# Copies of the identity into PSUM tiles at norms, write strengths' columns and latent vectors

## The chip, the cores and the metric

The kernel runs on one core of a Trainium2 chip. The metric is the device time of one execution in microseconds (us), and the time of a kernel is the median of its runs. A core has a matmul engine (TensorE, PE in the profile; its weight loads have a row of their own, PEld), three engines for element-wise work (VectorE is DVE, ScalarE is ACT, GpSimd is POOL) and a queue engine that issues most of the transfers (SyncE is SP). The engines run their own instruction streams in order and wait for each other by semaphores. Matmul results go to PSUM, all other data on chip stand in SBUF.

## What is computed

The input is a sequence of 256 tokens with 1024 features, all in float32. Two blocks follow one another. The first has a gated delta rule layer and a latent attention layer, each with a SwiGLU layer behind it; the second has two layers with four small mixers each and a SwiGLU layer with a causal convolution behind each. In short:

```python
def first_block(x, ...):
    for i in range(2):
        h = rms_norm(x, norm_mix[i])
        mix = gdn_mixer(h, ...) if i == 0 else mla_mixer(h, positions, ...)
        x = x + mix
        x = x + swiglu(rms_norm(x, norm_ffn[i]), ffn_w_gate_up[i], ffn_w_down[i])
    return rms_norm(x, final_norm)

def gdn_mixer(h, ...):
    proj = h @ w_in                 # q, k, v through a convolution, z, b, a
    beta = sigmoid(b)               # write strengths
    g = -exp(a_log) * softplus(a + dt_bias)   # decays, summed up along a chunk
    ...

def mla_mixer(h, ...):
    c_q, c_kv, k_rope = split(h @ w_in)       # 384, 256 and 64 columns: latent vectors
    q  = rms_norm(c_q, q_norm_g) @ w_q_up
    kv = rms_norm(c_kv, kv_norm_g) @ w_kv_up
    ...
```

The second block's norms are the same, with a scale and a shift per feature that come from a condition vector.

## The kernel before

The 256 tokens stand in two halves of 128 (t = 0 and 1), tokens on partitions. The layers run as stages one after the other: `g` (gated delta rule), `f0` (SwiGLU), `a` (latent attention), `f1` (SwiGLU), `m0` (mixers), `f2` (convolution and SwiGLU), `m1`, `f3`. In the profiled execution they begin at about 0, 298, 484, 598, 788, 968, 1180 and 1361 us.

Every large matmul is made of three: each operand is split into a high and a low part (`h_hi`, `h_lo` for activations, `wh`, `wl` for weights), and high times high, low times high and high times low are added in PSUM. `mm3_a` (L480, L483) has the weights as the stationary operand, `mm3_b` (L492 to L494) the activations. Weights are streamed: SP loads a raw 128x1024 tile, ACT makes `wh` of it (L464), and DVE (L469) or POOL (L467), as a table says, makes `wl`.

A norm works in this way for each half t. The sums of squares come from ACT, a Newton iteration of small instructions on DVE (L527 to L534) gives `rstd`, and DVE makes `xn` in two pieces of 512 columns (L601). TensorE transposes each piece into a PSUM tile `ps_t` of four 128x128 blocks (L611, transposes with the identity `ident`). In `m0`, `f2`, `m1` and `f3`, where a shift is added, it first puts the shift into the tile by one matmul with 512 columns (L604) and adds the blocks with plain float32 matmuls (L609). ACT reads the tile to make `h_hi` (L614) and DVE to make `h_lo` (L615), and the next stage's matmuls (`ps_gt` in the SwiGLU stages, `ps_ck` and `ps_cq` in `a`, `ps_lk` in `m1`) read those. One plain float32 matmul of the program is two matmuls in the trace, and a transpose is one.

In `g`, DVE makes the running sums of the decays, `gc`, by a scan (L854); four small matmuls (L896 for `beta`, L897 for `gc`) turn them and the write strengths into columns of the tile `ps_bg`, which DVE copies out (L898, L899). Between them in TensorE's queue stand the projection's matmuls into `ps_g`.

In `a`, the latent vectors of half t stand in the PSUM tiles `ps_ck` and `ps_cq`. ACT sums their squares (L1253), a Newton iteration on DVE (L507 to L521) gives `m_rs`, DVE scales both into `cn` (L1256), TensorE transposes five blocks (L1259, into `ps_ct`), ACT and DVE split them into `ck` and `cq` (L1189, L1190), and the values `ps_v` follow.

The order on each engine comes from a scheduler that places the instructions of the program by their dependencies and by priorities: a block under `high_priority(n)` moves ahead of its place (the first half of a norm does, by `np` of the stage's plan), and under `issue_after(x)` an instruction is not placed before x. All PSUM tiles named here come from one pool, `pm`.

Of the kernel before, what the change touches and what calls it, by code (L numbers as in the profile page):

```python
# [37 lines left out]
        w='PPPVPPPPPVPPPPPVPPPPPVPPPPPVPPPPPVPPPPPVPPPPPVPPPPVPPPVPPPVVVVVVV',  # L38
        pre=3,
        out=(0, 4, True),  # L40
# [337 lines left out]
class Prog:  # L378
    def __init__(self, ctx, tc, ap):
        self.tc, self.nc, self.ap = tc, tc.nc, ap  # L380
        nc = self.nc
        self.const = ctx.enter_context(tc.tile_pool(name="const", bufs=1, reuse_waits="tile"))
        self.xp = ctx.enter_context(tc.tile_pool(name="xp", bufs=1, reuse_waits="tile"))
        self.raw = ctx.enter_context(tc.tile_pool(name="raw", bufs=RAWB, reuse_waits="tile"))
        self.wsp = ctx.enter_context(tc.tile_pool(name="wsp", bufs=WSB, reuse_waits="tile"))
        self.hp = ctx.enter_context(tc.tile_pool(name="hp", bufs=1, reuse_waits="tile"))
        self.sm = ctx.enter_context(tc.tile_pool(name="sm", bufs=3, reuse_waits="tile"))
        self.pa = ctx.enter_context(tc.tile_pool(name="pa", bufs=4, space=PSUM, reuse_waits="tile"))
        self.dr = ctx.enter_context(tc.tile_pool(name="dr", bufs=1, space=DRAM))
        self.nw = 0  # L390
        self.more = None
        self.ready = []
        self.last_copy = self.last_raw = None
        self.mods = {}
        self.rstd = {}
        self.scaled = {}
        self.ada_todo = [(l, c) for l in range(2) for c in range(24)]
        self.ada_held = None
        self.behind = None
        self.spare = []  # L400

        self.ident = self.const.tile([128, 128], F32, name="ident")
        make_identity(nc, self.ident)
        self.small = self.const.tile([128, SMALL.n], F32, name="small")
        self.one = self.const.tile([128, 1], F32, name="one")
        nc.vector.memset(self.one, 1.0)
        self.nhalf = self.const.tile([128, 4], F32, name="nhalf")
        nc.vector.memset(self.nhalf, -0.5)
# [63 lines left out]
    def mm3_a(self, ps, w, kt, width, m0, m, x):  # L472

        nc = self.nc
        (wh, wl), (xh, xl) = w, x
        n = 0
        last = 3 * kt - 1
        for k in range(kt):
            for xx in (xh, xl):
                nc.tensor.matmul(ps, wh[:, k * width + m0 : k * width + m0 + m], xx[:, k, :], start=(n == 0), stop=(n == last))  # L480
                n += 1
        for k in range(kt):
            self.last_mm = nc.tensor.matmul(ps, wl[:, k * width + m0 : k * width + m0 + m], xh[:, k, :], start=False, stop=(n == last))  # L483
            n += 1

    def mm3_b(self, ps, lhs, w, sl, start, stop, shared=False):

        nc = self.nc
        wh, wl = w
        xh, xl = lhs  # L490
        kw = dict(skip_group_check=True) if shared else {}
        nc.tensor.matmul(ps, xh, wh[:, sl], start=start, stop=False, **kw)  # L492
        nc.tensor.matmul(ps, xl, wh[:, sl], start=False, stop=False, **kw)  # L493
        nc.tensor.matmul(ps, xh, wl[:, sl], start=False, stop=stop, **kw)  # L494

    def rsqrt(self, out, src, shape, scale, eps, pool=None, tag=None, bufs=1, key=""):

# [90 lines left out]
    def _norm(self, x, h, l, shift, xns):  # L588
        nc = self.nc
        with ExitStack() as st:  # L590
# [3 lines left out]
            for t in range(2):  # L594
# [4 lines left out]
                with self.tc.high_priority(self.plan["np"]) if t == 0 and self.plan["np"] else ExitStack():  # L599
                    for i, hv in enumerate(halves):  # L600
                        nc.vector.scalar_tensor_tensor(xn[:, hv], scaled[i] if scaled else x[:, t, hv], rstd, self.row[:, hv], op0=ALU.mult, op1=ALU.mult)  # L601
                        ps = self.pm.tile([128, 4, 128], F32, name="ps_t", tag="mm")
                        if shift:
                            nc.tensor.matmul(ps, self.row[:, D:], self.ident[:, 4 * i : 4 * i + 4].unsqueeze(2).to_broadcast([128, 4, 128]), start=True, stop=False, skip_group_check=True)  # L604
                        for j in range(4):
# [175 lines left out]
    def _gdn_core(self, x, dr, gi, vb, rq, zs, inner):  # L781
# [105 lines left out]
        with tc.tile_pool(name="g_rk", bufs=1, reuse_waits="tile") as pr:  # L887
# [2 lines left out]
            next(kp)  # L890

            ps = self.pm.tile([128, 2, 2, 16], F32, name="ps_bg", tag="mm")
            with tc.issue_after(self.last_mm.ins):
                for n in range(2):
                    sl = slice(n * 128, n * 128 + 128)
                    nc.tensor.transpose(ps[:, 0, n, :], beta[:, sl], self.ident[0:16, 0:16])  # L896
                    nc.tensor.transpose(ps[:, 1, n, :], gc[:, sl], self.ident[0:16, 0:16])  # L897
# [294 lines left out]
    def mla(self, x):  # L1192
        nc, tc, ap = self.nc, self.tc, self.ap
        with ExitStack() as fs:
# [50 lines left out]
            for t in range(2):  # L1245
# [5 lines left out]
                with tc.high_priority(MP):  # L1251
# [3 lines left out]
                    for i, (ps, n, gain, dst) in enumerate(parts):  # L1255
                        nc.vector.tensor_scalar(cn[i][:, : n * 128], ps, rs[:, i : i + 1], None, op0=ALU.mult)  # L1256
                        pt = self.pm.tile([128, n, 128], F32, name="ps_ct", tag="mm")
                        for k in range(n):
                            nc.tensor.transpose(pt[:, k, :], cn[i][:, k * 128 : k * 128 + 128], self.ident)  # L1259
                        self.split_t(pt, n, gain, dst[0][:, :, tk], dst[1][:, :, tk])  # L1260
# [1021 lines left out]
```

## Time and profile before

| what | value |
|---|---|
| median of 3 runs | 1563.18 us (1561.58 to 1564.20) |
| the profiled execution | 1564.72 us |
| its span in the trace | 1563.0 us |
| TensorE's mean granted clock in it | 0.976 |
| PE busy, share of the span | 1456.9 us, 93% |
| DVE, ACT, POOL busy | 1080.7, 811.3, 680.6 us |

The span is the time from the first to the last instruction in the trace; the 1.7 us that the execution took beyond it lie around it. TensorE is busy for 93% of the span, and the rest is spread over some dozens of waits of a few microseconds. Its clock has two levels, 2.4 GHz (1.00 in the tables) and 1.2 GHz (0.50); the trace shows which was granted in a stretch.

### The profile page before, as it was taken

Reading aid. Unit: us, or ns where it says so; the run is one execution under the profiler, and the core shown is the slowest. Engines: PE = TensorE matmul, PEld = TensorE weight load, DVE = VectorE, ACT = ScalarE, POOL = GpSimd, SP = SyncE. Lnnn points to the kernel's source line nnn. Section 1 sums busy time; section 2 is a strip of 40 time slices with the busy share of each in tenths; the row PEclk is TensorE's granted clock in tenths of the full one; section 3 lists DMA queues with packets and bytes.
Section 4 is the critical chain, followed back from the end, with each engine's and each line's share of the span. In section 5 each row is a group of like instructions: output and inputs, shape, how many; then the busy total and the mean of one; then the engine's idle time right before and its main releaser. Section 6 shows DMA issues by size and latency. Waiting matters only on the chain.

```text
span 1563.0 us, 25562 instructions
## 1 busy us (share of the span) xinstructions
PE 1456.9 (93%) x9582; PEld 1284.4 (82%) x9582; DVE 1080.7 (69%) x2094; ACT 811.3 (52%) x1476; POOL 680.6 (44%) x471
## 2 busy tenths in 40 slices
PE   5999999899999899999998989998999797999998
PEld 4988887699987787999877766898888675699987
DVE  3587646777677566997477577788975866776652
ACT  4675555544543464554355664555544465566651
POOL 3566734245442431543145432365535523236530
PEclk9999999999999999999999999999999998999999
DMA  4655522677784455888544314777764441375550
GB/s 160 228 169 171 188 83 71 212 282 285 285 315 132 136 175 185 320 317 297 185 138 139 110 60 126 269 255 261 279 239 153 137 115 55 122 257 177 196 186 37
DMA packets 104300, 293.34 MB, mean 188 GB/s; under 512 B 28104, under 2 KB 39024, under 8 KB 98032
## 3 DMA queue, kind: packets, MB, share of 16 engines
q1 hardware_dynamic: 94928, 237.51, 45.0%
q10 hardware_dynamic: 8896, 53.14, 9.3%
q8 instruction: 75, 1.23, 0.3%
q0 software_dynamic: 352, 1.06, 0.2%
q14 instruction: 49, 0.40, 0.1%
HBM read 288.43 MB, written 3.24 MB: 187 GB/s over the span
## 4 chain that ended last, share of the span: by engine, by line
PE 54%; DVE 12%; DMA 5%; issue 4%; ACT 4%; POOL 3%; SPq 0%; ACTq 0%; POOLq 0%; DVEq 0%
PE ps_gu L480 15%; PE ps_gu L483 7%; PE ps_o L493 7%; PE ps_o L494 7%; PE ps_o L492 7%; DVE wl L469 3%; ACT wh L464 1%; POOL wl L467 1%; DVE gu_u L2236 1%; DVE ada_raw L1402 1%; DMA raw<-in_u_gu 1%; DMA ada_raw<-in_ada 1%; DVE xn L601 1%; PE ps_bs L1991 1%; DMA raw<-in_f_gu 1%
## 5 line engine op out<-in xcount | busy, mean ns | idle before, releaser
L467 POOL TENSOR_TENSOR wl<-raw,wh 128x1024 fp32r<-128x1024 f32 (+4 forms) x162 | 401.3, 2484 | 381.5 <-ACT wh L464 340.9
L464 ACT CAST wh<-raw 128x1024 fp32r<-128x1024 f32 (+3 forms) x421 | 423.6, 1018 | 247.5 <-PE ps_o L493 95.9
L469 DVE TENSOR_TENSOR wl<-raw,wh 128x1024 fp32r<-128x1024 f32 (+2 forms) x259 | 355.8, 1382 | 113.8 <-ACT wh L464 113.0
L480 PE MATMUL ps_gu<-h_hi,wh 128*128 128x256 f32 x1280 | 314.1, 283 | 8.0 <-DVE gu_u L2236 8.0
L480 PE MATMUL ps_gu<-h_lo,wh 128*128 128x256 f32 x1280 | 313.7, 283 | 0.0
L480 PEld LDWEIGHTS ps_gu<-h_hi,wh 128*128 128x128 f32 x1280 | 245.6, 192 | 8.8 <-issue 8.7
L480 PEld LDWEIGHTS ps_gu<-h_lo,wh 128*128 128x128 f32 x1280 | 245.8, 192 | 0.2
L1402 DVE CUSTOM_DVE_ANT_0 ada_raw<-ada_raw,ada_cond 128x1024 f32<-128x1024 f32 x96 | 170.9, 1795 | 65.6 <-DMA ada_raw<-in_ada 65.6
L483 PE MATMUL ps_gu<-h_hi,wl 128*128 128x256 f32 x1280 | 179.2, 283 | 3.3 <-POOL wl L467 3.2
L483 PEld LDWEIGHTS ps_gu<-h_hi,wl 128*128 128x128 f32 x1280 | 164.2, 191 | 4.2 <-POOL wl L467 3.9
L493 PE MATMUL ps_o<-wh,act_l 128*128 128x512 f32 x352 | 138.6, 394 | 0.0
L494 PE MATMUL ps_o<-wl,act_h 128*128 128x512 f32 x352 | 138.5, 394 | 0.0
L492 PE MATMUL ps_o<-wh,act_h 128*128 128x512 f32 x352 | 138.2, 393 | 0.0
L2236 DVE SCALAR_TENSOR_TENSOR gu_u<-ps_gu,f2s,gu_u 128x254 f32<-128x254 f32 (+1 forms) x176 | 81.3, 476 | 40.8 <-ACT gu_u L2234 38.8
L744 POOL TENSOR_TENSOR act_l<-gu_t,act_h 128x256 fp32r<-128x256 f32 x44 | 54.9, 1250 | 108.5 <-ACT act_h L743 108.5
L2239 POOL TENSOR_TENSOR gu_t<-gu_t,gu_u 128x256 f32<-128x256 f32 x44 | 49.2, 1118 | 85.7 <-DVE gu_u L2236 83.0
L494 PEld LDWEIGHTS ps_o<-wl,act_h 128*128 128x128 f32 x352 | 66.1, 188 | 15.3 <-issue 0.5
L492 PEld LDWEIGHTS ps_o<-wh,act_h 128*128 128x128 f32 x352 | 66.1, 188 | 15.1 <-issue 0.2
L493 PEld LDWEIGHTS ps_o<-wh,act_l 128*128 128x128 f32 x352 | 66.1, 188 | 14.9 <-issue 0.2
L480 PE MATMUL ps_g<-h_hi,wh 128*128 128x256 f32 x256 | 66.2, 294 | 1.5 <-ACT wh L464 1.5
L743 ACT CAST act_h<-gu_t 128x256 fp32r<-128x256 f32 x44 | 17.7, 406 | 96.0 <-DVE gu_t L742 96.0
L2240 ACT CAST act_h<-gu_t 128x256 fp32r<-128x256 f32 x44 | 17.9, 407 | 94.8 <-POOL gu_t L2239 94.5
(663 smaller groups left out, 2976.4 us busy)
## 6 DMA issues: line engine op xcount, KB each, us to landing
ada_raw<-in_ada ACTq DMA_DIRECT2D x48, 1024.0 KB, 6.8
raw<-in_f_gu SPq DMA_DIRECT2D x88, 512.0 KB, 4.8
raw<-in_u_gu SPq DMA_DIRECT2D x88, 512.0 KB, 4.4
raw<-in_f_dn SPq DMA_DIRECT2D x44, 512.0 KB, 5.5
raw<-in_u_dn SPq DMA_DIRECT2D x44, 512.0 KB, 4.3
raw<-in_g_qkv SPq DMA_DIRECT2D x32, 512.0 KB, 3.5
raw<-in_g_z SPq DMA_DIRECT2D x16, 512.0 KB, 4.6
raw<-in_g_out SPq DMA_DIRECT2D x16, 512.0 KB, 3.5
```

What stands on the lines that cost most here:

```text
L464: self.last_copy = nc.scalar.copy(wh[:, :cols], raw[:, :cols])
L467: nc.gpsimd.tensor_tensor(wl[:, :cols], raw[:, :cols], wh[:, :cols].bitcast(F32), op=ALU.subtract)
L469: nc.vector.tensor_tensor(wl[:, :cols], raw[:, :cols], wh[:, :cols].bitcast(F32), op=ALU.subtract)
L480: nc.tensor.matmul(ps, wh[:, k * width + m0 : k * width + m0 + m], xx[:, k, :], start=(n == 0), stop=(n == last))
L483: self.last_mm = nc.tensor.matmul(ps, wl[:, k * width + m0 : k * width + m0 + m], xh[:, k, :], start=False, stop=(n == last))
L492: nc.tensor.matmul(ps, xh, wh[:, sl], start=start, stop=False, **kw)
L493: nc.tensor.matmul(ps, xl, wh[:, sl], start=False, stop=False, **kw)
L494: nc.tensor.matmul(ps, xh, wl[:, sl], start=False, stop=stop, **kw)
L744: nc.gpsimd.tensor_tensor(al[:, m, :], t, ah[:, m, :].bitcast(F32), op=ALU.subtract)
L1402: nc.vector.tensor_tensor_reduce(raw[:, j], raw[:, j], self.cond, 1.0, 0.0, op0=ALU.mult, op1=ALU.add, accum_out=mod[:, i : i + 1])
L2236: nc.vector.scalar_tensor_tensor(u[:, j, d:], ps[:, j, : S - d], cw[:, 3 * q + 2 - d : 3 * q + 3 - d], u[:, j, d:], op0=ALU.mult, op1=ALU.add)
L2239: nc.gpsimd.tensor_tensor(t, t, u[:, 0], op=ALU.mult)
```

## The change

A new helper `busy` issues n matmuls whose two operands are the identity, into a PSUM tile that is written again right after; nothing reads what they wrote. `self.last_any` is the last matmul that `mm3_a` or `mm3_b` has issued in program order, and the copies are not placed ahead of it. They stand at three kinds of place:

- each norm, ahead of the first transposes of t = 0: 8 copies of 128x128. The first norm of the program has no matmul before it and gets none, so there are 7 such places (`f0`, `a`, `f1`, `m0`, `f2`, `m1`, `f3`);
- the write strengths' columns, ahead of the four matmuls into `ps_bg`: 12 copies of 128x64;
- the latent vectors, ahead of the first transposes of t = 0 into `ps_ct`: 17 copies of 128x128.

That is 85 matmuls of the program, all plain float32.

```diff
         for k in range(kt):
-            self.last_mm = nc.tensor.matmul(ps, wl[...], xh[:, k, :], start=False, stop=(n == last))
+            self.last_mm = self.last_any = nc.tensor.matmul(ps, wl[...], xh[:, k, :], start=False, stop=(n == last))
...
-        nc.tensor.matmul(ps, xh, wl[:, sl], start=False, stop=stop, **kw)
+        self.last_any = nc.tensor.matmul(ps, xh, wl[:, sl], start=False, stop=stop, **kw)
+
+    def busy(self, out, n, after):
+
+        w = out.shape[-1]
+        with self.tc.issue_after(after.ins):
+            for _ in range(n):
+                self.nc.tensor.matmul(out, self.ident, self.ident[:, :w], start=True, stop=True, skip_group_check=True)
...
                         ps = self.pm.tile([128, 4, 128], F32, name="ps_t", tag="mm")
+                        if t == i == 0 and self.last_any:
+                            self.busy(ps[:, 0, :], 8, self.last_any)
                         if shift:
...
             ps = self.pm.tile([128, 2, 2, 16], F32, name="ps_bg", tag="mm")
+            self.busy(ps.rearrange("p a b c -> p (a b c)"), 12, self.last_mm)
             with tc.issue_after(self.last_mm.ins):
...
                         pt = self.pm.tile([128, n, 128], F32, name="ps_ct", tag="mm")
+                        if t == i == 0:
+                            self.busy(pt[:, 0, :], 17, self.last_any)
                         for k in range(n):
                             nc.tensor.transpose(pt[:, k, :], cn[i][:, k * 128 : k * 128 + 128], self.ident)
```

The scheduler places some neighbours anew. TensorE's queue in `g`, at the write strengths' columns, has before:

```order
L483 MATMUL ps_g<-h_hi,wl 128x256 x8
L896 MATMUL ps_bg<-ident,beta 128x16
L480 MATMUL ps_g<-h_hi,wh 128x256
L897 MATMUL ps_bg<-ident,gc 128x16
L896 MATMUL ps_bg<-ident,beta 128x16
L480 MATMUL ps_g<-h_lo,wh 128x256
L897 MATMUL ps_bg<-ident,gc 128x16
L480 MATMUL ps_g<-h_hi,wh 128x256
```

and now (L480 has become L481, L896 has become L907):

```order
L484 MATMUL ps_g<-h_hi,wl 128x256 x8
L502 MATMUL ps_bg<-ident 128x64 x12
L907 MATMUL ps_bg<-ident,beta 128x16
L908 MATMUL ps_bg<-ident,gc 128x16
L907 MATMUL ps_bg<-ident,beta 128x16
L908 MATMUL ps_bg<-ident,gc 128x16
L481 MATMUL ps_g<-h_hi,wh 128x256
```

The copies stand behind the group of `ps_g` that came before, the four small matmuls behind the copies, and the two matmuls of the next group that stood among them are behind them now.

TensorE's queue in `a`, at the latent vectors of t = 0 (`ps_ck` and `ps_cq` here are the last products of t = 1), has before:

```order
L494 MATMUL ps_ck<-wl,h_hi 128x320
L492 MATMUL ps_cq<-wh,h_hi 128x384
L1259 MATMUL ps_ct<-ident,cn 128x128 x2
L493 MATMUL ps_cq<-wh,h_lo 128x384
L494 MATMUL ps_cq<-wl,h_hi 128x384
L1259 MATMUL ps_ct<-ident,cn 128x128 x3
L492 MATMUL ps_ck<-wh,h_hi 128x320
L493 MATMUL ps_ck<-wh,h_lo 128x320
L494 MATMUL ps_ck<-wl,h_hi 128x320
L492 MATMUL ps_cq<-wh,h_hi 128x384
L493 MATMUL ps_cq<-wh,h_lo 128x384
L494 MATMUL ps_cq<-wl,h_hi 128x384
```

and now:

```order
L493 MATMUL ps_ck<-wh,h_hi 128x320
L494 MATMUL ps_ck<-wh,h_lo 128x320
L495 MATMUL ps_ck<-wl,h_hi 128x320
L493 MATMUL ps_cq<-wh,h_hi 128x384
L494 MATMUL ps_cq<-wh,h_lo 128x384
L495 MATMUL ps_cq<-wl,h_hi 128x384
L502 MATMUL ps_ct<-ident 128x128 x17
L1272 MATMUL ps_ct<-ident,cn 128x128 x5
```

Before, eight products of t = 1 stood behind the first transposes; now all of them stand ahead of the copies, and the five transposes follow in one piece.

At the norm of `f3`, TensorE's queue has before, in one piece at t = 0:

```order
L604 MATMUL ps_t<-ident,row 128x512 x4
L609 MATMUL ps_t<-ident,xn 128x128 x8
```

and now, at t = 0:

```order
L502 MATMUL ps_t<-ident 128x128 x8
L614 MATMUL ps_t<-ident,row 128x512
L619 MATMUL ps_t<-ident,xn 128x128 x4
L614 MATMUL ps_t<-ident,row 128x512
L619 MATMUL ps_t<-ident,xn 128x128 x4
```

The four shift matmuls, which stood together ahead of t = 0, are now one ahead of each piece, two of them at t = 1. The norms of `f2` and `m1` change alike (three shift matmuls and one a little later in `f2`), and in `a` and `m0` the last matmuls of the stage before, which stood among the transposes or the shift matmuls, now stand ahead of the copies.

## Rows read from the trace of the kernel before

**Rows 1.** The page's first part: busy time, share of the span, instructions.

```profile
PE 1456.9 (93%) x9582; PEld 1284.4 (82%) x9582; DVE 1080.7 (69%) x2094; ACT 811.3 (52%) x1476; POOL 680.6 (44%) x471
```

**Rows 2.** Stretches: start:end, length, busy per engine (instructions), granted clock, DMA share, GB/s.

```profile
320.00:484.00 164.00, 164.00 (x1182) 154.81 (x1181) 119.45 (x123) 71.08 (x102) 81.42 (x43) 1.00 0.76 279
1000.00:1120.00 120.00, 108.71 (x890) 107.13 (x889) 110.43 (x146) 65.16 (x109) 73.90 (x48) 0.97 0.72 262
1380.00:1540.00 160.00, 160.00 (x1161) 152.21 (x1160) 98.13 (x134) 93.25 (x145) 74.64 (x55) 1.00 0.55 180
```

**Rows 3.** The same view, stretches in which the granted clock is half.

```profile
45.30:52.20 6.90, 5.58 (x25) 5.28 (x26) 4.05 (x10) 2.05 (x4) 0.17 (x1) 0.51 0.59 198
301.30:304.80 3.50, 3.50 (x12) 2.52 (x11) 2.86 (x9) 2.48 (x5) 0.00 (x0) 0.51 0.53 199
315.00:318.40 3.40, 3.40 (x9) 2.64 (x8) 0.64 (x1) 1.92 (x2) 0.00 (x0) 0.50 0.95 299
519.80:526.60 6.80, 5.36 (x18) 4.88 (x19) 4.44 (x23) 2.56 (x9) 0.24 (x1) 0.50 0.20 60
608.50:612.00 3.50, 3.50 (x11) 2.51 (x10) 1.58 (x3) 3.47 (x4) 0.00 (x0) 0.51 0.80 295
```

**Rows 4.** PE's timeline: start, duration, line, operands, shape, count [idle before, releaser].

```profile
120.66 0.51 PE L868 MATMUL pss<-fi,sq 128*128 128x16 f32 x4
...
970.67 3.60 PE L604 MATMUL ps_t<-ident,row 128*128 128x512 f32 x8
974.52 2.05 PE L609 MATMUL ps_t<-ident,xn 128*128 128x128 f32 x16 [0.25 <-DVE xn L601]
```

**Rows 5.** PE's timeline at the write strengths' columns in `g`.

```profile
41.92 1.12 PE L483 MATMUL ps_g<-h_hi,wl 128*128 128x256 f32 x8
...
46.62 0.28 PE L897 MATMUL ps_bg<-ident,gc 16*128 16x16 f32 x1 [3.11 <-DVE gc L854]
...
50.82 1.71 PE L483 MATMUL ps_g<-h_hi,wl 128*128 128x256 f32 x8
52.37 0.28 PE L480 MATMUL ps_g<-h_hi,wh 128*128 128x256 f32 x1
```

**Rows 6.** Timelines of PE and DVE at the latent vectors in `a`.

```profile
521.24 0.69 PE L1259 MATMUL ps_ct<-ident,cn 128*128 128x128 f32 x2 [5.77 <-DVE cn L1256]
...
524.76 0.63 PE L492 MATMUL ps_v<-wh,ck 128*128 128x512 f32 x1
...
528.52 1.07 PE L1259 MATMUL ps_ct<-ident,cn 128*128 128x128 f32 x5
...
514.95 1.60 DVE L507 TENSOR_SCALAR rs_v<-m_ss 128x2 f32<-128x2 f32 x1 [4.12 <-ACT cn L1253]
...
525.62 0.17 DVE L507 TENSOR_SCALAR rs_v<-m_ss 128x2 f32<-128x2 f32 x1 [0.46 <-ACT cn L1253]
```

**Rows 7.** Timelines of PE and DVE at the norm of `f0`.

```profile
300.86 1.69 PE L611 MATMUL ps_t<-ident,xn 128*128 128x128 f32 x8 [2.22 <-DVE xn L601]
...
313.67 0.63 PE L611 MATMUL ps_t<-ident,xn 128*128 128x128 f32 x4 [2.18 <-DVE xn L601]
...
308.14 5.38 DVE L601 SCALAR_TENSOR_TENSOR xn<-x_t,rstd,row 128x512 f32<-128x512 f32 x2
```

**Rows 8.** PE's timeline at the norms of `a`, `f1`, `m0`, `m1` and `f3`.

```profile
503.53 0.42 PE L494 MATMUL ps_ck<-wl,h_hi 128*128 128x320 f32 x1 [1.06 <-DVE wl L469]
...
597.83 1.03 PE L611 MATMUL ps_t<-ident,xn 128*128 128x128 f32 x8
...
607.14 1.32 PE L611 MATMUL ps_t<-ident,xn 128*128 128x128 f32 x8 [1.82 <-DVE xn L601]
...
797.69 1.49 PE L609 MATMUL ps_t<-ident,xn 128*128 128x128 f32 x11 [2.49 <-DVE xn L601]
...
1185.46 2.05 PE L609 MATMUL ps_t<-ident,xn 128*128 128x128 f32 x16 [0.58 <-DVE xn L601]
...
1365.29 2.42 PE L609 MATMUL ps_t<-ident,xn 128*128 128x128 f32 x16 [0.30 <-DVE xn L601]
```

More of the change, by code (lines that the diff above doesn't have):

```diff
@@ L392, in __init__ @@
         self.ready = []
+        self.last_any = None
         self.last_copy = self.last_raw = None
@@ L482, in mm3_a @@
         for k in range(kt):
-            self.last_mm = nc.tensor.matmul(ps, wl[:, k * width + m0 : k * width + m0 + m], xh[:, k, :], start=False, stop=(n == last))
+            self.last_mm = self.last_any = nc.tensor.matmul(ps, wl[:, k * width + m0 : k * width + m0 + m], xh[:, k, :], start=False, stop=(n == last))
             n += 1
```

## Prediction

> **What bounds the kernel now.** I read the page's first part first: TensorE is busy for 1456.9 of 1563.0 us [rows 1], so whatever is gained or lost must show up on TensorE, as idle time, as slow time, or as added work. Then I read long stretches of the SwiGLU stages: in `f0` and from 1380 us on TensorE is busy for all of 164.00 and 160.00 us [rows 2], so a shift in time ahead of these stages, in either direction, goes through them to the end. `f2` is different: between 1000 and 1120 us TensorE is busy for 108.71 and VectorE for 110.43 of 120 us [rows 2], so a microsecond more or less on TensorE just before it can vanish there. Third, the granted clock. It falls to its lower level in five stretches near the places that the change touches [rows 3]: once behind the write strengths' columns (6.90 us long), twice in `f0` (3.50 and 3.40), once behind the latent vectors (6.80) and once in `f1` (3.50). In each of them TensorE has just waited, or is waiting, for VectorE: 3.11 us for `gc` [rows 5], 2.22 and 2.18 us for `xn` [rows 7], 5.77 us for `cn` [rows 6], 1.82 us for `xn` [rows 8]. So each wait is paid twice: as idle time, and then as slow matmuls. The copies can save only the second part: they do nothing to make `gc`, `xn` or `cn` come earlier.
>
> **The price of a copy.** Sixteen plain float32 matmuls of 128x128 (8 of the program) take 2.05 us, and their starts lie about 0.118 us apart [rows 4]. So 8 copies are 1.9 us and 17 are 4.0 us of TensorE's time. For the 64-column copies no row has the shape. From below the four matmuls with 16 columns bound it, at 0.51 us or some 0.11 us apart [rows 4]; from above the 128-column pitch of 0.118. I take 0.11, since so few columns leave the weight load as the limit: 24 matmuls in 2.65 us (2.6 to 2.85). A shift matmul (L604, two in the trace) is a quarter of 3.60 us, 0.9 us [rows 4]. The seven norms, 17 and 12 copies add up to 20.0 us of TensorE's time; the question is how much of that lies in waits.
>
> **Write strengths' columns.** The group of `ps_g` ahead ends at about 43 us (it starts at 41.92 and is 1.12 long), and `gc` releases TensorE at 46.62 [rows 5]. The copies fill 2.65 of that and are over by 45.7: they cost nothing. The next group of `ps_g` runs in the slow stretch. Eight of its matmuls take 1.71 us there and 1.12 at the full clock [rows 5]; the difference is over seven distances, 0.084 us each, so 24 matmuls lose 2.0 us. If the clock stays up, the group that starts at 52.37 starts 2.0 us earlier. The four small matmuls also come ahead of the group, so the columns are copied out a little earlier. What is late next is the decay chain of the gated delta rule, which waits on other engines now and then; I keep −2.0 and allow 0 to −2.5, since a part can be lost in these waits, and another order in `g` can cost as well.
>
> **`f0`.** The copies (298.6 to 300.5) fit in the wait of 2.22 us, which ends at 300.86 [rows 7]. The slow stretch behind it [rows 3] costs up to half its length, 1.7 us. But t = 1 takes this back: its two `xn` pieces take 5.38 us on VectorE from 308.14 on, and TensorE waits 2.18 us for the second, to 313.67 [rows 7]. That time is VectorE's and the weight split's beside it; a faster TensorE only waits longer. I take 0 (−1.0 to +1.5; the upper end if a longer wait also makes the second slow stretch longer).
>
> **`a`, the norm.** Here `xn` was there before TensorE was free: the transposes stood among the last products of the stage before, and there is no wait to fill. So 1.9 us of copies lie bare. Next on the path is the wait of 1.06 us for a `wl` tile at 503.53 [rows 8], which takes most of that back. +0.5 (0 to +1.6).
>
> **`a`, the latent vectors.** The wait of 5.77 us lasts from 515.47 to 521.24 [rows 6]. Eight products of t = 1 stood behind the first transposes; they take about 1.2 us at full clock and now fill the head of the wait. The 17 copies then take 4.0 us: 515.5 + 1.2 + 4.0 = 520.7, just before `cn` is there. Behind it, between 521.24 and 524.76, before had those products and the five transposes at half clock, 3.5 us; now only the transposes are left, and the values can start once `ck` is split, about 1.3 us after. That would be a gain of 2.2 us, and the first values at the full clock some 1 us more. The next wait is `cn` of t = 1: its Newton iteration started at 525.62 when its squares were there [rows 6], and those wait for the products that now come 8 us earlier; VectorE starts it once the first half's work is done, 2 to 2.5 us earlier than now. So −2.4 (−4.0 to −1.0).
>
> **`f1`.** The transposes at 597.83 follow without a wait [rows 8]: 1.9 us bare. At t = 1, the wait of 1.82 us to 607.14 [rows 8] takes this back, but for VectorE's order, in which `xn` of t = 1 comes some tenths later. With the wait filled by work, the slow stretch at 608.5 should go, up to 1.75 us [rows 3]. −1.2 (−1.7 to +1.9).
>
> **The second block.** No slow stretch follows its norms, so there is nothing to win, only work that may not fit. `m0`: the wait is 2.49 us [rows 8], and the last products move ahead of the copies; they fit, +0.3 for VectorE's order (0 to 0.6). `f2`: the four shift matmuls filled the wait for `xn` but for 0.25 us [rows 4]; with 1.9 us of copies ahead, one shift matmul falls behind the first products: +1.0, of which the slack of `f2` [rows 2] takes most; +0.2 (0 to 1.0). `m1`: the wait was 0.58 us [rows 8]; copies of 1.9 us, less the shift matmul that moved away (0.9), leave the second piece 0.4 to 1.2 us later; +0.7. `f3`: the wait was 0.30 us [rows 8] because four shift matmuls filled it. Now copies and two of them do, and the other two (1.8 us) go to t = 1, where TensorE has no slack; the first piece's earlier transposes give a little back: +1.2 (0 to 1.9).
>
> **Sum.** −2.0 + 0 + 0.5 − 2.4 − 1.2 + 0.3 + 0.2 + 0.7 + 1.2 = −2.7 us. On the profiled execution, 1564.72, that is 1562.0; this execution was 1.5 above the median, and I forecast the median: 1563.18 − 2.7 = 1560.5.
>
> **The rivals.** *All slow stretches pay in full.* The columns give 2.3, `f0` 1.0, the latent vectors 3.2 and `f1` 1.5, and the costs of the other places come to 1.0 net, because VectorE is what they wait for anyway: −7.0, 1556.2. For it: each stretch follows directly on a wait that the copies fill. Against: t = 1 of `f0` and the bare copies.
>
> *The copies stand in front of operands that are already there* (slower). At `a`, `f1`, `f2`, `m1` and `f3` there is little or no wait at t = 0; if no later wait takes their time back, they cost 1.6 + 1.9 + 1.0 + 1.2 + 1.9 = 7.6, and with half of the clock's gain at the columns and the latent vectors (−2.8) the sum is about +4.8: 1568.0. It decides from the point where `xn` is ready more than about 1 us before the copies end and no wait of that size comes within the next 10 us. Against: the waits of 1.06 and 1.82 us that do come [rows 8].
>
> *The clock falls all the same, here or elsewhere.* In the trace the wait of 2.22 us at `f0` was followed by a slow stretch and the longer one of 2.49 us at `m0` was not [rows 3, 7, 8], so the length of a wait alone doesn't decide. If as much time is slow as before, the columns give 0, `f1` +0.3 (1.9 bare, less 1.82 of wait, and some tenths of VectorE), the latent vectors keep only their eight products, −1.2, and the costs stay at 2.9: +2.0, 1565.2. The Trainium skill, in "TensorE: Matmul & The Clock Gate", Part 1, section "What's actually happening", says that how many slow matmuls a kernel sees varies from run to run with the phase of the activity monitor. By that rule a shift of the program could move the slow stretches to places that have none now; the two waits above fit it, and this is the page's case against the change.
>
> *The gain stays where it is made.* The columns' and the latent vectors' gain is lost in waits for VectorE within their own layer, the costs are absorbed too: about −0.5, 1562.7.
>
> **How the numbers follow.** Chances: the forecast 0.45 (1558.5 to 1562.5), all stretches pay 0.20, copies in front of ready operands 0.14, the clock falls all the same 0.11, the gain stays 0.10. The 80% range leaves out the ends of the first two rivals: 1556.0 to 1567.0. The measurement can tell about 0.2%, 3.1 us: faster is below 1560.0, slower above 1566.3. From the forecast 0.21 is faster and 0.24 the same; all stretches pay is faster; of ready operands 0.13 is slower; the clock's case is the same but for 0.02 slower; the last is the same. Faster 0.41, same 0.44, slower 0.15.
>
> **What would show it.** Right: the granted clock is 1.00 between 45 and 52 and between 520 and 527 us; the group of `ps_g` that started at 52.37 starts at about 50.4; the values start near 522.5; the slow stretch at 608 is gone; `f0`'s t = 1 wait is longer than before; and from the start of `f2` to the end of the kernel the trace is 1 to 3 us longer. Wrong: new slow stretches behind places that had none, a wait in `g` that eats the 2 us, or the first matmuls behind the norms of `a` and `f1` late by 1.9 us with no shorter wait behind them.

## The result and the profile after

The changed kernel is slower: 1572.93 us in the median of 20 runs (1566.28 to 1577.87), beside 1561.93 us for the kernel before (20 runs, 1553.67 to 1568.44). The ratio is 1.0072, with a 95% interval of 1.0061 to 1.0083: +11.2 us (9.5 to 13.0). A second measurement gave 1.0089 (1.0067 to 1.0111). The forecast was −2.7 us, and the range ended at 1567.0. Single runs of one kernel differ by several microseconds here; the profiled execution of the changed kernel has a span of 1569.5 us, so a trace shows a part of the loss and not always the same part.

The page's first part, of the changed kernel (compare [rows 1]):

```profile
PE 1464.8 (93%) x9752; PEld 1298.8 (83%) x9752; DVE 1075.1 (69%) x2094; ACT 811.8 (52%) x1476; POOL 673.5 (43%) x471
```

TensorE has 170 more matmuls (9752 for 9582), as worked out, but is busy for only 7.9 us more, and its mean granted clock is higher: 0.983 for 0.976 in these traces, 0.981 for 0.978 in the mean of 20 and 35 runs. Its idle time, which is the span less its busy time, hardly changed: 104.7 us for 106.1. So the waits that the copies filled came back as other waits. The stretches of [rows 3] in the changed kernel (same columns):

```profile
45.30:52.20 6.90, 5.92 (x36) 5.63 (x36) 4.61 (x12) 3.65 (x7) 0.19 (x1) 0.75 0.62 193
301.30:304.80 3.50, 3.06 (x23) 2.54 (x21) 3.29 (x10) 0.99 (x3) 0.00 (x0) 1.00 0.75 265
519.80:526.60 6.80, 6.80 (x54) 6.80 (x53) 3.05 (x17) 0.00 (x0) 0.24 (x1) 1.00 0.09 37
608.50:612.00 3.50, 2.10 (x10) 1.40 (x8) 3.46 (x4) 1.62 (x3) 2.08 (x1) 1.00 0.89 284
```

Three of the four are at the upper level now, and the first is slow for half of its length. Not all of this comes from the copies: the traces of the experiments below show which stretches move by themselves (see the part on why the prediction was wrong). And one stretch in `g` is slow that was not: before, then now:

```profile
215.60:222.40 6.80, 6.80 (x75) 5.89 (x72) 3.40 (x10) 3.86 (x13) 1.94 (x3) 1.00 0.01 2
215.60:222.40 6.80, 6.14 (x40) 5.48 (x39) 3.06 (x10) 3.03 (x11) 1.21 (x2) 0.50 0.35 99
```

What TensorE waits for (line, waited for: us in total, times, longest us), in the changed kernel:

```profile
PE pss L878 <- ACT sq L891: 3.9, 2, 3.5
...
PE ps_gt L494 <- DVE h_lo L625: 3.1, 4, 1.8
...
PE ps_rp L1191 <- DVE four L1189: 2.1, 1, 2.1
...
PE ps_ck L494 <- DVE h_lo L625: 1.9, 1, 1.9
```

The first and the last two are new; the wait for `h_lo` ahead of `ps_gt` was 1.6 us in total before, 0.7 at the longest. To see where the time went I matched every matmul of the changed kernel's trace with its namesake in the trace of before (same tiles and shape, counted in order) and took the difference of the starts. It stands at −0.8 at 60 us, −0.1 at 140 and still at 185, +2.7 at 188, +5.2 at 230, +3.3 at 280 (all in `g`), +1.0 in the middle of `f0`, +6.7 at 510 and +3.6 at 540 (both in `a`), +4.1 in `f1`, +4.5 in `m0`, +3.4 in `f2`, +4.5 in `m1`, and +6.5 from 1380 us, in `f3`, to the end. So the losses are made in `g`, in `a` and in `f3`. The zero of this scale is uncertain: ten of the kernels below have no copies ahead of 290 us, and their difference at 60 us lies between −0.3 and −2.4. Only steps within a stage count.

At the norm of `a` (timelines of PE, then DVE):

```profile
497.29 1.95 PE L502 MATMUL ps_t<-ident 128*128 128x128 f32 x16
499.07 1.04 PE L621 MATMUL ps_t<-ident,xn 128*128 128x128 f32 x8
...
502.80 0.42 PE L494 MATMUL ps_ck<-wh,h_lo 128*128 128x320 f32 x1 [1.87 <-DVE h_lo L625]
...
496.17 1.42 DVE L609 SCALAR_TENSOR_TENSOR xn<-x_t,rstd,row 128x512 f32<-128x512 f32 x2
...
498.10 1.68 DVE L470 TENSOR_TENSOR wl<-raw,wh 128x704 fp32r<-128x704 f32 x2
...
499.82 1.59 DVE L1169 TENSOR_SCALAR ang<-fi,pf 128x32 f32<-128x32 f32 x1
...
502.08 1.27 DVE L625 TENSOR_TENSOR h_lo<-ps_t,h_hi 128x512 fp32r<-128x512 f32 x2
...
509.90 2.30 DVE L1189 COPY four<-ct 128x256 f32<-128x256 f32 x1 [0.68 <-ACT ct L1185]
```

GpSimd's weight splits in the same time:

```profile
499.69 1.68 POOL L468 TENSOR_TENSOR wl<-raw,wh 128x704 fp32r<-128x704 f32 x1 [7.31 <-ACT wh L465]
509.69 2.35 POOL L468 TENSOR_TENSOR wl<-raw,wh 128x1024 fp32r<-128x1024 f32 x1 [8.32 <-PE ps_cq L495]
```

and VectorE's same instructions before:

```profile
497.28 0.69 DVE L615 TENSOR_TENSOR h_lo<-ps_t,h_hi 128x512 fp32r<-128x512 f32 x1 [0.70 <-ACT h_hi L614]
...
500.07 0.23 DVE L1158 TENSOR_SCALAR ang<-fi,pf 128x32 f32<-128x32 f32 x1
...
508.20 0.28 DVE L1178 COPY four<-ct 128x256 f32<-128x256 f32 x1
```

`xn` is there at 497.6, and the copies stand in front of the transposes until 499.1, as forecast. What was not forecast is behind it: two weight splits, the first instruction of the rotary tables (`ang`) and eight small instructions, of the tables and of the Newton iteration of t = 1, now stand ahead of both pieces of `h_lo` on VectorE, and TensorE waits another 1.87 us. Order is not all of it. `ang` starts inside a weight split of GpSimd, ends with it and takes 1.59 us for 0.23 before; `four`, the rotary table for which TensorE then waits 2.10 us, starts inside the next split, ends 0.2 us behind it and takes 2.30 for 0.28. At the latent vectors:

```profile
522.53 0.61 DVE L1267 TENSOR_SCALAR cn<-ps_cq,m_rs 128x384 f32<-128x384 f32 x1
...
523.32 3.96 PE L502 MATMUL ps_ct<-ident 128*128 128x128 f32 x34
527.11 0.71 PE L1272 MATMUL ps_ct<-ident,cn 128*128 128x128 f32 x5
528.32 0.73 PE L493 MATMUL ps_v<-wh,ck 128*128 128x512 f32 x2 [0.49 <-ACT ck L1200]
```

Where TensorE waited 5.77 us for `cn` [rows 6], there is no wait any more: the products end at 523.3, `cn` is ready at 523.1, and all 17 copies stand in front of operands that are there. The clock is up, and the 3.96 us are lost. The wait went in two ways: the products end later, and the Newton iteration, which had 1.60 and 2.24 us long instructions in it before, now runs without them (from 519.36 to 521.50).

### The profile page after: what moved, and what is told of

Read it like the earlier page. It is cut to its first block, busy times and chain, and to the rows that moved or that the text cites. A ratio compares the mean times of both kernels' runs of the same rounds, so it can differ in the third digit from the quotient of the medians.

```text
span 1569.5 us, 25903 instructions
## 1 busy us (share of the span) xinstructions
PE 1464.8 (93%) x9752; PEld 1298.8 (83%) x9752; DVE 1075.1 (69%) x2094; ACT 811.8 (52%) x1476; POOL 673.5 (43%) x471
## 4 chain that ended last, share of the span: by engine, by line
PE 53%; DVE 15%; DMA 5%; issue 4%; ACT 4%; POOL 2%; SPq 0%; ACTq 0%; POOLq 0%; DVEq 0%
PE ps_gu L481 15%; PE ps_gu L484 7%; PE ps_o L494 6%; PE ps_o L495 6%; PE ps_o L493 6%; DVE wl L470 4%; DVE ada_raw L1415 2%; ACT wh L465 1%; DVE gu_u L2249 1%; DMA raw<-in_u_gu 1%; DMA ada_raw<-in_ada 1%; DMA raw<-in_w_d 1%; DVE xn L609 1%; PE ps_bs L2004 1%; PE ps_u L481 1%
## 5 line engine op out<-in xcount | busy, mean ns | idle before, releaser
L481 PE MATMUL ps_gu<-h_hi,wh 128*128 128x256 f32 x1280 | 314.6, 284 | 8.6 <-DVE gu_u L2249 8.6
L481 PE MATMUL ps_gu<-h_lo,wh 128*128 128x256 f32 x1280 | 313.9, 284 | 0.0
L481 PEld LDWEIGHTS ps_gu<-h_hi,wh 128*128 128x128 f32 x1280 | 246.5, 193 | 9.6 <-issue 9.4
L481 PEld LDWEIGHTS ps_gu<-h_lo,wh 128*128 128x128 f32 x1280 | 246.7, 193 | 0.2
L2252 POOL TENSOR_TENSOR gu_t<-gu_t,gu_u 128x256 f32<-128x256 f32 x44 | 45.7, 1039 | 94.1 <-DVE gu_u L2249 86.6
L495 PEld LDWEIGHTS ps_o<-wl,act_h 128*128 128x128 f32 x352 | 66.2, 188 | 14.9
L753 ACT CAST act_h<-gu_t 128x256 fp32r<-128x256 f32 x44 | 17.7, 406 | 101.7 <-DVE gu_t L752 101.7
L481 PE MATMUL ps_g<-h_hi,wh 128*128 128x256 f32 x256 | 65.0, 290 | 0.0
L481 PE MATMUL ps_g<-h_lo,wh 128*128 128x256 f32 x256 | 64.3, 287 | 0.0
```

The costliest lines, as they stand in the source:

```text
L495: self.last_any = nc.tensor.matmul(ps, xh, wl[:, sl], start=False, stop=stop, **kw)
L2252: nc.gpsimd.tensor_tensor(t, t, u[:, 0], op=ALU.mult)
```

## Experiments

Theory A: the scheduler counts the copies as time and lets other work of VectorE pass ahead of what the norms need. Theory B: the loss is in `g`. Theory C: the copies' own time is the cost. The edits are shown against the changed kernel, if nothing else is said; "us" are the ratio's difference from 1, times 1562.

**The three kinds of place apart.** `norms` has no copies at the columns and the latent vectors, `bg` has only the columns' and `ct` only the latent vectors'.

```diff
# norms
-            self.busy(ps.rearrange("p a b c -> p (a b c)"), 12, self.last_mm)
-                        if t == i == 0:
-                            self.busy(pt[:, 0, :], 17, self.last_any)
# bg: without the lines of the norms and the latent vectors
# ct: without the lines of the norms and the columns
```

> Only the seven norms get their copies (8 each); the write strengths' columns and the latent vectors get none. Theory A (VectorE's order): the loss is made at the norms, where other work of VectorE now stands ahead of h_lo, above all in stage a (+5.6 us between 494 and 512 us in the changed kernel's trace) and in f3 (+2.5 between 1368 and 1383), less some 2 us won in f0. So +8 to +12 us against the kernel before. Theory B (the gated delta rule): the loss is made in g by the moved matmuls, so the norms alone come to at most +4 us.

> Only the write strengths' columns get their 12 copies. 172 instructions of TensorE and 51 of VectorE move in g. Theory A: -1 to +1 us, since the 0.8 us won by 60 us are given back by 140 us. Theory B: +3 to +6 us, what the changed kernel's trace shows as added between 180 and 240 us.

> Only the latent vectors get their 17 copies; eight products move ahead of them. Both theories: -2 to -4 us, with the granted clock at its upper level between 516 and 526 us and the values starting 2 us or more earlier. If the gain is the products' order alone and not the clock, -1.2 us.

Measured: `norms` 1.0018 (1.0001 to 1.0035), +2.8 us; `bg` 1.0015 (1.0000 to 1.0029), +2.3; `ct` 0.9975 (0.9964 to 0.9986), −3.9. `norms` missed theory A's +8 to +12 and lies within theory B's bound of +4; `bg` lies between A's −1 to +1 and B's +3 to +6. Neither theory is borne out in these sizes. The three sum to +1.2, the changed kernel is at +11.2: the parts work against each other. In the trace of `norms` the late norm of `a` costs nothing in the end (the difference is +5.2 at 515 us and −2.2 at 530): the wait at the latent vectors takes it back.

**Copies of one column.** `w1` keeps all 85 copies, one column wide:

```diff
-                self.nc.tensor.matmul(out, self.ident, self.ident[:, :w], ...)
+                self.nc.tensor.matmul(out[:, :1], self.ident, self.ident[:, :1], ...)
```

> The same 85 copies at the same places, but of one column each instead of 128 or 64. The planner counts these as nearly nothing and leaves almost all of the old order (25 instructions of VectorE stand elsewhere, against 103 with the full copies); on the chip each still loads its weights, so TensorE should be held for 85 x 2 x 0.11 = 18.7 us in all. Theory A: near the kernel before, -2 to +3 us. If the copies' own time is what costs (theory C), +7 to +11 us, as in the changed kernel.

Measured: 1.0014 (1.0001 to 1.0026), +2.2 us. In the trace the eight copies of a norm hold TensorE for 1.84 us and the 17 for 3.85, as long as the full ones, while nearly all of the order is the old one. The first part of its page:

```profile
PE 1469.8 (94%) x9752; PEld 1300.8 (83%) x9752; DVE 1079.2 (69%) x2094; ACT 809.8 (52%) x1476; POOL 678.8 (43%) x471
```

TensorE is busy for 12.9 us more than before and idle for 91.2 us of a span of 1561.0, 14.9 less: with the old order the copies do fill waits, where in the changed kernel the idle time stayed. Across the norm of `a` the difference grows by 1.8 us here and by 5.7 in the changed kernel. So the time that the copies take on TensorE is not what makes +11: theory C falls. (They also don't hold the clock as the full ones do; see the end.)

**The norm of `a` and the latent vectors.** `a_and_ct` has the copies at these two places only; `a_and_ct_one` has 8 and 1, `ct_one` only 1 and `ct_nine` only 9 at the latent vectors:

```diff
-                            self.busy(pt[:, 0, :], 17, self.last_any)
+                            self.busy(pt[:, 0, :], 1, self.last_any)
```

> Copies at the norm of stage a (8) and at the latent vectors (17) alone. If the two places add up, about -4 us: the latent vectors alone gave a ratio of 0.9975, and in the trace with the copies at all norms the late norm of a is taken back by the wait for the latent vectors (-0.5 us at 490, -2.2 at 530). If they work against each other (the late norm eats the wait, and the 17 copies then stand in front of latent vectors that are ready), +1 to +4 us, with 17 copies in one piece, no wait behind them, and the values starting 2 to 4 us later than in the kernel before.

> Copies at the norm of stage a (8) and a single one at the latent vectors in place of 17; but for it the order is almost that of the run with both (four instructions of VectorE differ). If the 17 copies stood bare in front of ready latent vectors, this is 4 us better than that run: 0 to +1.5 us against the kernel before. If the late norm of a is the cost by itself, it stays at +3 to +5.

Measured: `a_and_ct` 1.0029 (1.0016 to 1.0042), +4.5 us; `a_and_ct_one` 0.9987 (0.9976 to 0.9998), −2.0. The 16 copies between them make 6.5 us by the runs, more than their 3.7 us; from the first product of `a` (`ps_ck`) to the rotary part of the keys (`ps_kp`) the two traces differ by 3.25 us (35.59 and 32.34), so the rest may be the width of the intervals. The timelines, `a_and_ct` first:

```profile
520.40 0.61 DVE L1268 TENSOR_SCALAR cn<-ps_cq,m_rs 128x384 f32<-128x384 f32 x1
...
521.20 3.96 PE L504 MATMUL ps_ct<-ident 128*128 128x128 f32 x34
524.99 0.71 PE L1273 MATMUL ps_ct<-ident,cn 128*128 128x128 f32 x5
```

and `a_and_ct_one`:

```profile
522.42 0.38 PE L504 MATMUL ps_ct<-ident 128*128 128x128 f32 x2
522.64 0.71 PE L1273 MATMUL ps_ct<-ident,cn 128*128 128x128 f32 x5
```

With 17, `cn` is ready at 521.0 and its transposes start at 525.0; with one they follow at once. So the late norm of `a` is harmless by itself (with one copy at the latent vectors), and the 17 copies win by themselves; together there is no wait left for the second to fill. That is shown. How much of the wait the late products use up, and how much goes because the Newton iteration no longer runs beside a split of GpSimd, no run separates.

> One copy instead of 17 at the latent vectors, nothing elsewhere. The eight products of t = 1 still move ahead of the transposes; the copies' work and what it does to the clock are left out. If the gain of the 17 copies is the clock, this one is at -1 us or less; if it is the products' order, -3 to -4 us like the 17. I expect -1.5 to -2.5, with a slow stretch in the 10 us behind the wait.

> Nine copies instead of 17 at the latent vectors, nothing elsewhere: 2.1 us of the wait instead of 4.0. One copy gave a ratio of 0.9991 and a slow stretch of 6.8 us, 17 gave 0.9975 and none. If half the wait filled is enough to keep the clock, -3 to -4 us; if not, -1 to -2 with a slow stretch behind the wait.

Measured: `ct_one` 0.9991 (0.9974 to 1.0008), −1.4 us; `ct_nine` 0.9975 (0.9962 to 0.9987), −3.9, like `ct`. The clock behind the wait, in `ct_one` and then in `ct`:

```profile
517.80:524.70 6.90, 3.88 (x12) 2.95 (x13) 5.78 (x27) 2.09 (x8) 1.03 (x2) 0.51 0.30 104
```

```profile
516.90:523.70 6.80, 4.29 (x20) 2.71 (x19) 5.53 (x27) 3.70 (x11) 0.24 (x1) 1.00 0.14 51
```

From the first product of `a` to the rotary part of the keys, the traces take 35.05 us before, 35.20 with one copy and 33.56 with 17. Other traces agree: 33.63 and 33.71 in the two further kernels with 17 copies and the old norm of `a` (`ct_bgcol`, `five_norms_ct`), neither of which is slow there, and 34.87 to 35.20 in those without copies (`bg`, `f3_alone`, `f3_pin`), each of which has a slow stretch of 6.8 us there. So the eight products' order brings nothing here, and the clock 1.5 us. The runs say −3.9, with −2.2 as the near end of the interval; the 0.7 us between and the gain of `ct_nine`, which still has a slow stretch of 3.4 us and 35.17 us for the same piece of its trace, are not settled.

**The norm of `f3`.** `f3_alone` has the copies at that norm only. `f3_pin` is the same, but one weight split (the seventh of the stage) is held behind `h_lo` (`self.last_lo` is the last instruction that made an `h_lo`):

```diff
         else:
-            nc.vector.tensor_tensor(wl[:, :cols], ...)
+            with self.tc.issue_after(self.last_lo.ins) if self.stage_name == "f3" and self.np == 7 else ExitStack():
+                nc.vector.tensor_tensor(wl[:, :cols], ...)
```

> Copies at the norm of f3 alone (8); of the order, four instructions of TensorE and two of VectorE move: two shift matmuls go to t = 1, and h_lo of t = 1 goes behind a weight split. Expected +2 to +4 us, all of it between 1360 and 1385 us, with a wait for h_lo at t = 1 of about 1.8 us. If the copies' own time were the cost, it would show as a later start of the first products of t = 0 instead, and come to at most +1.9.

> The kernel with copies at the norm of f3 alone, and one thing undone: the weight split that had come in front of h_lo of t = 1 on VectorE is held behind it again. The copies and the two shift matmuls at t = 1 stay. If h_lo's place in VectorE's queue is the cost, the wait of 1.76 us for h_lo is gone and the kernel is 1.5 to 2.5 us better than f3 alone, +1 to +3 us against the kernel before. If the shift matmuls and the copies are the cost, it stays at +4 to +6.

Measured: `f3_alone` 1.0032 (1.0018 to 1.0045), +5.0 us; `f3_pin` 1.0004 (0.9993 to 1.0016), +0.6. In the trace of `f3_alone` the difference goes from −2.4 to +1.0 within the stage, in that of `f3_pin` it grows by 1.1. DVE before the change:

```profile
1376.32 1.29 DVE L615 TENSOR_TENSOR h_lo<-ps_t,h_hi 128x512 fp32r<-128x512 f32 x2 [0.69 <-ACT h_hi L614]
1377.76 1.60 DVE L469 TENSOR_TENSOR wl<-raw,wh 128x1024 fp32r<-128x1024 f32 x1
```

DVE and then PE, of `f3_alone`:

```profile
1374.86 2.55 DVE L472 TENSOR_TENSOR wl<-raw,wh 128x1024 fp32r<-128x1024 f32 x1 [1.15 <-ACT wh L467]
1377.33 1.28 DVE L627 TENSOR_TENSOR h_lo<-ps_t,h_hi 128x512 fp32r<-128x512 f32 x2
...
1371.54 1.02 PE L616 MATMUL ps_t<-ident,row 128*128 128x512 f32 x2
...
1373.30 1.02 PE L616 MATMUL ps_t<-ident,row 128*128 128x512 f32 x2
...
1378.06 0.50 PE L496 MATMUL ps_gt<-wh,h_lo 128*128 128x512 f32 x1 [1.76 <-DVE h_lo L627]
```

and of `f3_pin`:

```profile
1367.68 0.69 DVE L628 TENSOR_TENSOR h_lo<-ps_t,h_hi 128x512 fp32r<-128x512 f32 x1 [1.64 <-ACT h_hi L627]
1369.11 0.69 DVE L628 TENSOR_TENSOR h_lo<-ps_t,h_hi 128x512 fp32r<-128x512 f32 x1 [0.74 <-ACT h_hi L627]
1369.72 6.98 DVE L473 TENSOR_TENSOR wl<-raw,wh 128x1024 fp32r<-128x1024 f32 x5
```

One weight split, which waits for its operand for 1.15 us and then takes 2.55, stands ahead of `h_lo`, and VectorE works through its queue in order. With the split behind it, VectorE makes each half of `h_lo` as soon as `h_hi` is there. Most of the cost of this norm is that one instruction's place: 4.4 us between the two ratios, more than the wait of 1.76 us in one trace; the shift matmuls and the copies come to +0.6.

**The columns.** `ct_bgcol` is `ct` with 12 one-column copies at the columns, which leaves the order in `g` as it was; `no_bg` is the changed kernel without the copies there.

```diff
# ct_bgcol
-            self.busy(ps.rearrange("p a b c -> p (a b c)"), 12, self.last_mm)
+            self.busy(ps.rearrange("p a b c -> p (a b c)")[:, :1], 12, self.last_mm)
```

> The 17 copies at the latent vectors, and at the write strengths' columns 12 copies of one column, which the planner counts as nothing, so that g keeps its old order. If the loss of the 12 full copies in g was the order, this is -4 to -5 us, at least as good as the latent vectors alone; if the copies themselves cost in g, -1 to -3.

> The changed kernel without the copies at the write strengths' columns. If their new order in g costs the 2 to 3.5 us that the trace shows, +8 to +11 us against the kernel before; if it is no cost in the whole, +12 to +14.

Measured: `ct_bgcol` 0.9986 (0.9973 to 1.0000), −2.2 us, not the −4 to −5; `no_bg` 1.0055 (1.0038 to 1.0072), +8.6. So the columns' copies cost 2.3 us alone and 2.6 within the whole, or 5.3 by the second measurement of the whole. In the traces of `bg` and of the changed kernel alike a wait comes up that before did not have (PE's timeline, `bg`):

```profile
107.69 0.62 PE L877 MATMUL pss<-fi,sq 128*128 128x16 f32 x4 [3.46 <-ACT sq L890]
```

It costs nothing in the end: at 100 us TensorE is 3 us further ahead of the kernel before than at 80, and at 110 the difference is within 0.3 us of where it was. But the difference grows by 5 to 6 us between 180 and 230 in both (and falls back by about 2 by 280), where in `ct_bgcol` it stays within 0.3 us. Of this, 2.8 us come at once at 188, and 3.4 between 210 and 225, where the slow stretch at 215.6 lies, which `bg` has too (214.9 to 221.7). The second trace of the changed kernel (`after_again`, below) has the first step and not the stretch:

```profile
215.60:222.40 6.80, 5.88 (x72) 5.27 (x72) 3.02 (x10) 4.82 (x19) 1.21 (x2) 1.00 0.35 95
```

It grows by 3.5 us to 230, and by 280 all three traces keep 2.7 to 3.5. That points at the moved order (172 instructions of TensorE move), but one-column copies are also less of a load; which of the moved instructions costs was not tried.

**The whole.** `after_again` is the changed kernel once more, `five_norms_ct` leaves out the three places (norms of `a` and `f3`, columns), and `mended` keeps all seven norms' copies but has one copy at the latent vectors, one-column copies at the columns, and the split pinned in `f3`.

> The changed kernel itself, once more, beside the three below on one chip. If the parts make the whole, it is +9 to +13 us: stage a with the latent vectors (+4.5), f3 (+5.0) and the write strengths' columns (+2.3) sum to +11.8. If the first measurement was a peculiarity of its chip, +3 to +8.

> The changed kernel without the three places that cost: no copies at the norms of a and f3 and none at the write strengths' columns; 17 at the latent vectors and 8 at the norms of f0, f1, m0, f2 and m1 stay. If the costs were those three places, -3 to -6 us, at least as good as the latent vectors alone. If the other norms cost too, -2 to +2.

> The changed kernel with three things undone and all seven norms' copies kept: one copy instead of 17 at the latent vectors (they stood bare), the weight split held behind h_lo of t = 1 in f3, and one-column copies at the write strengths' columns (old order in g). If these three make up the loss, +0 to +3 us against the kernel before, from the small costs of the other norms. If something else makes up half of it, +5 us or more.

Measured: `after_again` 1.0089 (1.0067 to 1.0111), +13.9 us; `five_norms_ct` 1.0004 (0.9992 to 1.0017), +0.6, a miss: beside `ct` (−3.9) the other five norms cost about 4.5 us; `mended` 1.0007 (0.9990 to 1.0025), +1.1. The three places by themselves, +4.5, +5.0 and +2.3, sum to +11.8, between the two measurements of the whole, and with all three undone little is left (−1.6 to +3.9 us). The sum has no room for 4.5 us of the five norms, and `norms` and `mended` leave less than that for them; with intervals of 2 to 3 us to either side their cost stays open. Theory A is shown at `f3`, where one pinned instruction takes most of the cost away. At the norm of `a` it rests on the traces and on `w1`; no run held `h_lo` in its place there. What costs in `g` is open.

The best version is the copies at the latent vectors alone (`ct`, or `ct_nine`): 0.9975, faster than both kernels by 2.0 us at least.

## Why the prediction was wrong

The prices of the copies held: 1.95 us for eight, 3.96 for 17, 2.79 for the 12 narrow ones (forecast 1.9, 4.0 and 2.65). What failed is the assumption behind every term, that the rest of the order costs only what TensorE's own queue shows, and with it the addition of the norm of `a` to the latent vectors. That pair was entered at +0.5 − 2.4 = −1.9 and measured +4.5; `f3` was entered at +1.2 and measured +5.0; the columns at −2.0 and +2.3. The three miss by 6.4 + 3.8 + 4.3 = 14.5 us, and the whole missed by 13.9.

The clock was forecast from one trace of the kernel before, and the other traces show how much of that was chance. At two places it did what was forecast. Behind the latent vectors no trace with 17 full copies in the wait is slow, and every trace with one copy or none and the old norm of `a` is. Behind t = 0 of `f0` all six traces with eight full copies there are free of the slow stretch that starts between 298 and 302 us in nine of ten without copies there. At the columns and in `f1` it was not the copies, as said below.

- **Columns**, forecast −2.0 (0 to −2.5). The stretch became slow later, for 3.4 us instead of 6.9, but that is no gain of the copies: of the ten kernels without copies ahead of 290 us, eight are slow there for 3.4 us as well and two for 6.8, and all are earlier than the kernel before at 60 us. So the 6.90 us was one of two lengths that come up, and nothing shows that the copies shortened it. The end above zero was left out of the range although "another order in `g` can cost as well" stood beside it: measured +2.3, with one of the forecast's own signs of being wrong, a new slow stretch at 215.6.
- **`f0`**, 0. The difference fell by 2.4 us across this norm in the changed kernel and rose by 1.1 in `norms`; in kernels without copies there it moves between −1.9 and +1.6. No sign.
- **Norm of `a`**, +0.5 (0 to +1.6). In the trace +5.7: the copies, then 1.87 us for `h_lo` behind other work of VectorE, then 2.10 us for the rotary tables; two instructions of VectorE that ran beside a split of GpSimd are 3.4 us longer than before and sit in these two waits. Six of the seven traces with this norm's full copies grow by 5.7 to 7.2 us here, one by 4.2. This is the step that failed first: I had the order of TensorE's queue before me and took VectorE's part of it as nothing.
- **Latent vectors**, −2.4. Alone this was right in sign and size (−3.9 by runs, −1.5 in the trace), though by the traces the products' order, which the third rival counts at −1.2, brought nothing. But the wait of 5.77 us was entered in the sum as if the term of the norm of `a` just before could not use it up. The two terms were added; they share one wait.
- **`f1`**, −1.2. Measured in the trace +0.6 (+0.6 to +1.8 over the kernels that have it). The slow stretch is gone, but so it is in six kernels without copies here, whose difference falls by 0.8 to 1.1 us across this norm; and the second trace of the changed kernel has it (609.8 to 613.2). So the copies cost their bare 1.8 us and the clock's gain is not theirs. The wait for `xn` of t = 1, which was to pay, is still 1.78 us: VectorE is later there too.
- **`m0`** +0.3, **`m1`** +0.7, **`f2`** +0.2: the trace gives +0.4, +0.7 and +0.9. `m1` is at +0.7 in all six traces with full copies and at 0 in all without: right. `f2` is at +1.3 by the end of the stage, up to +3.8 in the other five, and between −0.4 and +1.9 without copies: it scatters, and was more likely too small.
- **`f3`**, +1.2 (0 to 1.9): +3.0 in the trace and +5.0 by runs alone. The two shift matmuls at t = 1 were seen; the split in front of `h_lo` was in VectorE's queue and was not costed.

Of the rivals, the one that came closest is "copies in front of operands that are already there", at 1568.0 with a chance of 0.14. It holds word for word at the latent vectors, where it expected half of the clock's gain, and at `f1`. It does not hold at the norms of `a` and `f3`: with VectorE's order kept (`w1`, `f3_pin`) copies in front of ready operands cost little there. "The clock falls all the same" fits what was seen of single stretches (`f0`'s moved to 309.9 to 316.8 us in `norms` and is gone in the changed kernel; 215.6 to 222.4 is slow in one trace of the changed kernel and not in the other) but not the result, since the mean clock rose. The Trainium skill says in "TensorE: Matmul & The Clock Gate", Part 1, section "What's actually happening", that the number of slow matmuls of one kernel varies from run to run with the phase of the activity monitor. The two traces of the changed kernel, slow for 53.4 and 46.3 us in all and at different places, agree with it; it was not what decided.

## What to carry to other kernels

Filler work in a kernel whose order a scheduler sets is not only time on its own engine: the scheduler takes it as time too and lets other engines' work pass ahead of what the filler delays, so the order has to be read on the engine behind (here VectorE's `h_lo`), and pinned if need be. A wait can be filled once: when two edits stand before the same wait, cost them together. A slow stretch seen in one trace may be missing in the next of the same code, so read it in several traces, also of kernels that don't touch the place, before a change is credited with its going. Filler belongs only where its end is ahead of the operand with room to spare, and a single place that is right, such as the latent vectors here, can be worth more than nine.

## What was not expected of the hardware

A busy TensorE did not always keep its clock. In `w1` it is busy without a gap from 514.0 us on, the 17 one-column copies among it, and is granted half the clock from 520.3 on:

```profile
514.00:520.30 6.30, 6.30 (x53) 6.30 (x52) 5.40 (x18) 0.00 (x0) 2.56 (x2) 1.00 0.47 155
520.30:523.70 3.40, 3.11 (x10) 2.25 (x9) 2.30 (x12) 2.45 (x9) 0.00 (x0) 0.50 0.00 0
```

Behind 17 full copies there none of seven traces is slow. At the columns, `ct_bgcol` with one-column copies is slow for 6.9 us:

```profile
45.10:52.00 6.90, 6.34 (x31) 6.15 (x32) 4.17 (x10) 2.14 (x4) 0.28 (x1) 0.51 0.55 186
```

but `w1`, with the same copies there, for 3.4, as are kernels with full copies or none. What makes the difference is not settled by these runs.

Also, the small instructions of a Newton iteration on VectorE, 0.16 us each, can take 2 us while POOL splits weights. Before, in the wait of 5.77 us:

```profile
514.15 4.86 POOL L467 TENSOR_TENSOR wl<-raw,wh 128x1024 fp32r<-128x1024 f32 x2 [2.07 <-ACT wh L464]
...
516.78 2.24 DVE L519 TENSOR_TENSOR rs_t<-rs_s 128x2 f32<-128x2 f32 x1
```

This one and the one of 1.60 us [rows 6] start inside one of the two splits and end with it, within 0.04 us, as `ang` does with its split in the changed kernel. How long such a wait is, and so how much filler fits, depends on where POOL's work happens to fall.
